# Queueing the third branch's weight sums early, and another split of the last output tile

## The chip, the cores and the metric

The kernel runs on one core of a Trainium2 chip. The metric is the device time of one execution in microseconds. The core has TensorE (PE in the profile) for matmuls, VectorE (DVE), ScalarE (ACT), GpSimd (POOL) and SyncE (SP); sixteen DMA engines move data between HBM and the on-chip memories. Here SP's queue loads weights and inputs, and POOL's queue carries transfers from HBM to HBM, some of which add to what stands at their destination.

## What is computed

One layer of an encoder on 512 tokens of width 1024, in float32. Three branches, each a half-width mixer of the same normalised input, are projected back to 1024 columns, weighted by sigmoid gates and summed; an output projection, a gated feed-forward part and a final norm follow.

```python
h = _rmsnorm(x, norm_mix[l])
p = h @ w_in[l]
u, v, bg, cg, xb, zc, gl = jnp.split(p, splits, axis=-1)
ya = _sgu(gelu(u), gelu(v), ...)
yb = bg * _causal_dwconv(cg * xb, conv_b_w[l])
yc = _pool_mixer(zc, pool_w[l], pool_scale[l])
g = jax.nn.sigmoid(gl).reshape(bn, s, N_BRANCH, D_MODEL)
merged = (g[:, :, 0] * (ya @ w_br_a[l])
          + g[:, :, 1] * (yb @ w_br_b[l])
          + g[:, :, 2] * (yc @ w_br_c[l]))
x = x + merged @ w_o[l]
h = _rmsnorm(x, norm_ffn[l])
a = _causal_dwconv(h @ w_up[l], ffn_conv_w[l])
ag, av = jnp.split(a, 2, axis=-1)
x = x + (silu(ag) * av) @ w_down[l]
return _rmsnorm(x, norm_f)
```

## The kernel before, in words

Every matmul is done in three passes: each operand is split into a rounded upper half and a remainder (`_hi`, `_lo`), and `mm3` (L81 to L83) multiplies upper by upper, upper by lower, lower by upper, 128 by 128 weights against 512 columns a time. Weights come from HBM in pieces of 512 KB, through SP's queue (L106), into a pool of raw buffers (at most four in use for the weights). ACT rounds a piece into `ring_hi` (L59, or L63 where the piece is negated), DVE takes the remainder into `ring_lo` (L67 or L64), and PE uses the pair. The ring has four slots, so the split of a piece waits for its load and for the product four pieces earlier to be through.

The order of the program is: the value input (`pv`), the columns of the input projection (`pu`, `pz`, `pcg`, `pxb`, `pbg`), then branch 0, gate 0, branch 1, gate 1, branch 2, gate 2 (`bx`, `bd`, `ba` for a branch; `gx`, `ga`, `gd` for a gate), the output projection (`po`), the feed-forward part (`pug`, `puv`) and the down projection (`dx` to `df`), whose tail scales the rows and stores them.

Branches, gates and the down projection are multiplied by Strassen's scheme: seven products of quarters in place of eight, of which four need sums of quarters of the weight. For the three gates, the third branch and the down projection these sums are made by DMA, without an engine: `WeightSums` (L135) keeps four tensors t1 to t4 in HBM, `copy` (L146) copies a quarter into each, and `add` (L151) adds another quarter, or an earlier sum, to it by an accumulating transfer. t2 gets t1 added to it, t4 gets t2. The first two branches make their sums on DVE from loaded quarters (`more`, L178).

POOL issues the sums' transfers in the order written (`in_order`). The sums of gates 0 and 1 are queued one after another at L635, once the value input is through. Those of the third branch (512 KB a transfer) and of gate 2 (1 MB a transfer) stand in a list, `behind` (L927 to L930), and `next_sum` takes one entry from it at certain products: ACT copies one column of the product's accumulator into a mark (L936), POOL copies that mark (L407, `passed`), and the transfers behind it start only then. `next_sum` is called after each of a gate's seven products, and, in branches 1 and 2, after the third product (L1039).

DVE and ACT work in the order written too. In a branch (L1028) the last product, `a22`, goes into the bank `x` that held `s3`, so it starts after DVE has taken `s3` out (L842). In the next branch's first steps, ACT copies `bx` (L951) into a scratch buffer that the gate before used for its last weighing on DVE (L842).

At the end, `finish` (L1216) scales a token tile of 1024 columns by its row factor `rstd`. Half of the columns is scaled by ACT and sent from ACT's queue (L1221, L1222); the other half by DVE and sent from SP's (L1225, L1228, L1229). In the last tile DVE does it in two pieces of 256 columns, of which one still needs the norm's gain.

Of the kernel before, what the change touches and what calls it, by code (L numbers as in the profile page):

```python
# [10 lines left out]
AF = mybir.ActivationFunctionType  # L11
ALU = mybir.AluOpType
# [7 lines left out]
NT = S // P  # L20
# [6 lines left out]
def trunk_kernel(  # L27
# [4 lines left out]
    nc = tc.nc  # L32
# [8 lines left out]
    def bank(name):  # L41
        return ps.tile([P, S], F32, tag="ps", name=name)

    def scratch(i, name, width=S):
        return scr.tile([P, 528], F32, tag=f"s{i}", name=name)[:, :width]
# [46 lines left out]
    class Raws:  # L92


        def __init__(self):
            self.todo, self.ready, self.live, self.cap = [], [], 0, 4
# [38 lines left out]
    class WeightSums:  # L135
        def __init__(self, name, b11, b12, b21, b22):
            t1, t2, t3, t4 = self.t = [
                dram.tile([P, b11.shape[1], 528], F32, name=f"{name}_t{i + 1}")[:, :, :512] for i in range(4)]
            self.base = [(t1, b11), (t3, b12), (t2, b22), (t4, b21)]
            self.added = [(t1, b12), (t3, b22), (t2, t1), (t4, t2)]  # L140

            self.products = {"m1": b11, "m2": b21, "m3": b22, "m4": t4, "m5": t1, "m6": t2, "m7": t3}

# [96 lines left out]
    def tiny(tag, name):  # L240
        return small.tile([P, 1], F32, tag=tag, name=name)
# [156 lines left out]
    def quarters(half, c0):  # L398
        return [half(k)[:, :, c0 + 512 * h:c0 + 512 * h + 512] for k in range(2) for h in range(2)]

    gate_sums = [WeightSums(f"g{i}", *quarters(lambda k: w_in_v[:, 4 * k:4 * k + 4], 3072 + 1024 * i))
                 for i in range(3)]
    last_branch_sums = WeightSums("br2", *quarters(lambda k: w_br_q[2][k], 0))

    def pool_waits_for(t, name):

        in_order(nc.gpsimd.tensor_copy(tiny(name, name), t[:, 0:1]))  # L407
# [25 lines left out]
    def load_gain(g, tags, name):  # L433

        halves = []
        for c in range(2):
            t = act.tile([P, S], F32, tag=tags[c], name=f"{name}{c}")
            nc.sync.dma_start(t, g[512 * c:512 * c + 512].partition_broadcast(P))
            halves.append(t)
        return halves  # L440
# [191 lines left out]
        v_gelu(t)  # L632
    v_center()
    pool_waits_for(pw_raw, "begun")
    for sums in gate_sums[:2]:  # L635
        sums.copy()
        sums.add()

# [25 lines left out]
    for b in range(2):  # L664
        w = blocks.take(f"u{b}")
        for j in range(2):
            o = bank(f"pu{b}{j}")
# [80 lines left out]
    for b in range(2):  # L748
        w = blocks.take(f"z{b}")
        for j in range(2):  # L750
            g = 2 * b + j
            o = bank(f"pz{g}")
# [7 lines left out]
    for b in range(2):  # L760
        w = blocks.take(f"cg{b}")
        cg = []
        for j in range(2):
            o = bank(f"pcg{b}{j}")
# [8 lines left out]
        for j in range(2):  # L773
            c = 2 * b + j
            o = bank(f"pxb{c}")
# [6 lines left out]
            a = scratch(1, f"cva{c}")  # L782
# [7 lines left out]
        for j in range(2):  # L790
            c = 2 * b + j
            o = bank(f"pbg{c}")
# [27 lines left out]
    def form(tags, name):  # L820

        return [[act.tile([P, 2, 256], F32R, tag=tags[2 * kp + i], name=f"{name}_{p}{kp}")
                 for i, p in enumerate(("hi", "lo"))] for kp in range(2)]
# [17 lines left out]
    def tt(o, a, b, op):  # L841
        nc.vector.tensor_tensor(o, a, b, op=op)  # L842
# [41 lines left out]
    sums = []  # L884
# [39 lines left out]
    nc.vector.tensor_scalar(nrstd1, rstd1, -1.0, None, op0=ALU.mult)  # L924


    behind = [lambda: last_branch_sums.copy()]  # L927
    behind += [lambda: last_branch_sums.add(1)] * 4
    behind += [lambda: gate_sums[2].copy(2)] * 2
    behind += [lambda: gate_sums[2].add(1)] * 4  # L930

    def next_sum(o):
        if behind:
            n = len(behind)
            mark = tiny(f"mark{n}", f"mark{n}")
            nc.scalar.copy(mark, o[:, 0:1])  # L936
            pool_waits_for(mark, f"passed{n}")
            behind.pop(0)()

    def product(o, st, n, first):  # L940
        for q in range(0, n, 2):
            [w] = pieces.take()
            for k in range(q, q + 2):
                mv = [p[:, 512 * (k - q):512 * (k - q) + 512] for p in w]
                for r in range(2):
                    mm3(o[r], st(k, r), mv, first and k == 0, k == n - 1, more=not first)

    def copies(tag, name, o):
        got = [scratch(tag, f"{name}{r}") for r in range(2)]
        for r in range(2):  # L950
            nc.scalar.copy(got[r], o[r])  # L951
        return got

    def banks(name):
        return [bank(f"{name}{r}") for r in range(2)]
# [72 lines left out]
    def branch(i, form):  # L1028
        c = [[act.tile([P, S], F32, tag=f"m{8 + 2 * t + h}" if i == 0 else f"x{t}{h}", name=f"c{i}{t}{h}")
              for h in range(2)] for t in range(NT)]  # L1030
        x = banks(f"bx{i}")
        product(x, form("a11"), 2, True)
        m1 = copies(0, f"bm1{i}", x)
        d = banks(f"bd{i}")
        product(d, form("s1"), 2, True)
        m5 = copies(1, f"bm5{i}", d)
        product(x, form("s2"), 2, False)
        if i > 0:
            next_sum(x[1])  # L1039
        m16 = copies(2, f"bm16{i}", x)  # L1040
        a = banks(f"ba{i}")
        product(a, form("a12"), 2, True)
        for r in range(2):
            tt(c[r][0], a[r], m1[r], ALU.subtract)
        product(x, form("s3"), 2, False)
        for r in range(2):
            tt(c[2 + r][1], x[r], m5[r], ALU.add)
        product(d, form("s4"), 2, False)
        for r in range(2):
            tt(c[r][1], d[r], m16[r], ALU.add)  # L1050
        product(x, form("a22"), 2, False)
        for r in range(2):
            nc.scalar.mul(c[2 + r][0], x[r], -1.0)
        return c

    for i in range(3):
        c = branch(i, forms[i])
        if i == 0:
            acc = c
        gate(i, c)  # L1060


    xr = [[act.tile([P, S], F32, tag=f"x{t}{c}", name=f"xr{t}{c}") for c in range(2)] for t in range(NT)]
# [11 lines left out]
    for h in range(2):  # L1075
        o = {}
# [88 lines left out]
    for b in range(NFF // 2):  # L1165
        w = blocks.take(f"ug{b}")
        ag = []
        o = [bank(f"pug{b}{j}") for j in range(2)]
# [13 lines left out]
        o = [bank(f"puv{b}{j}") for j in range(2)]  # L1182
# [6 lines left out]
    out_t = out[0].rearrange("(t p) d -> t p d", p=P)  # L1189

    def tail_rstd(ss, name):

        n = ss.shape[-1] - 1
        b = eps_t
        for i in range(n):
            b2 = tiny(f"b{i % 2}", f"{name}_b{i}")
            nc.vector.scalar_tensor_tensor(
                b2, ss[:, i:i + 1], 1.0 / D, b, op0=ALU.mult, op1=ALU.add)
            b = b2
        nb = tiny("nb", f"{name}_nb")  # L1200
        nc.vector.tensor_scalar(nb, b, -0.5, None, op0=ALU.mult)
        r = tiny("rr", f"{name}_r")
        nc.scalar.activation(r, ss[:, n:n + 1], AF.Sqrt, scale=1.0 / D, bias=b)
        h = tiny("rh", f"{name}_h")
        nc.vector.scalar_tensor_tensor(h, ss[:, n:n + 1], -0.5 / D, nb, op0=ALU.mult, op1=ALU.add)
        y = tiny("ry", f"{name}_y")
        nc.vector.reciprocal(y, r)
        t = tiny("rt", f"{name}_t")
        nc.vector.scalar_tensor_tensor(t, y, h, y, op0=ALU.mult, op1=ALU.mult)
        y2 = tiny("rz", f"{name}_z")  # L1210
        nc.vector.scalar_tensor_tensor(y2, t, 1.5, y, op0=ALU.add, op1=ALU.mult)
        return y2
# [3 lines left out]
    def finish(t):  # L1216

        h = int(t < 2)
        rstd = tail_rstd(ssf[t], f"hf{t}")
        xs = xr[t][1 - h]  # L1220
        nc.scalar.activation(xs, xs, AF.Copy, scale=rstd)  # L1221
        nc.scalar.dma_start(out_t[t][:, 512 * (1 - h):512 * (1 - h) + 512], xs)  # L1222
        a = 0 if t < NT - 1 else 256
        xs = xr[t][h][:, a:]
        nc.vector.scalar_tensor_tensor(xs, xs, rstd, gain3[h][:, a:], op0=ALU.mult, op1=ALU.mult)  # L1225
        if a:
            xs = xr[t][h][:, :a]
            nc.vector.tensor_scalar(xs, xs, rstd, None, op0=ALU.mult)  # L1228
        nc.sync.dma_start(out_t[t][:, 512 * h:512 * h + 512], xr[t][h])  # L1229

    def add_up(t, h, i, cut=slice(0, 512), gain=True):

# [49 lines left out]
    x = banks("dx")  # L1282
# [4 lines left out]
    gain3 = load_gain(norm_f, (g_tags[40], g_tags[41]), "gain_f")  # L1287
# [12 lines left out]
    a = banks("da")  # L1300
# [13 lines left out]
    for r in range(2):  # L1314
        tt(xr[r][1], d[r], m16[r], ALU.add)
        add_up(r, 1, 1, gain=False)
        finish(r)
# [5 lines left out]
    for qs in ([0], [2], [4, 6, 8, 10]):  # L1323
        ws = taken(qs)
        for r in range(2):
            t = 2 + r
            for i, (cut, o) in enumerate(zip(cuts[r], f[r])):
                o = o[:, :cut.stop - cut.start]
# [37 lines left out]
```

## Time and profile before

| | us |
|---|---|
| median of 3 runs (lowest, highest) | 739.06 (738.57, 740.81) |
| profiled execution: its own time | 736.67 |
| profiled execution: span from first to last instruction | 734.9 |
| PE busy in the span | 720.7 |
| DVE busy, ACT busy, POOL busy | 562.7, 370.6, 62.6 |

PE is the busiest engine. The page's busy time says nothing of stops by itself: the list of waits tells what PE waited for, the table by stretches tells where, and the chain of work and the timelines tell why. The profiled execution lies 2.4 us under the median of the runs, and 1.9 us under the lowest.

### The profile page before, as it was taken

How to read it: one execution, taken by the hardware profiler on the slowest of the kernel's cores; microseconds unless marked ns; L12 is line 12 of the kernel's file. 1: busy time of each engine (PE TensorE's matmuls, PEld its weight loads, DVE VectorE, ACT ScalarE, POOL GpSimd, SP SyncE). 2: the span in 40 equal slices, each digit the busy share in tenths (PEclk: the TensorE clock that was granted, in tenths of full speed). 3: DMA queues.
4: the chain of work that ended last, by engine and by line, in shares of the span. 5: the costliest groups of instructions: out<-in, count | busy, mean ns of one | idle time of the engine just before them, and what ended most of it. 6: DMA issues, size and time to landing. Idle time of an engine off the chain costs nothing.

```text
span 734.9 us, 8928 instructions
## 1 busy us (share of the span) xinstructions
PE 720.7 (98%) x3258; PEld 594.8 (81%) x3258; DVE 562.7 (77%) x836; ACT 370.6 (50%) x551; POOL 62.6 (9%) x93
## 2 busy tenths in 40 slices
PE   8999999999999998999999999999999999999996
PEld 5888888888877886888888888888888888888885
DVE  6889899889598687677556786766787776997674
ACT  4744144266675565664444443443444444965453
POOL 0041210001221100000012010100000000000110
PEclk9999999999999999999999999999999999999999
DMA  8649999737999996675228999999633232576652
GB/s 254 192 170 283 244 331 237 183 90 232 304 313 313 229 295 199 196 225 183 87 75 264 236 296 285 253 311 220 178 97 105 86 106 82 155 234 201 194 163 114
DMA packets 89211, 150.87 MB, mean 205 GB/s; under 512 B 4008, under 2 KB 39248, under 8 KB 89168
## 3 DMA queue, kind: packets, MB, share of 16 engines
q1 hardware_dynamic: 68607, 96.76, 41.7%
q0 software_dynamic: 19840, 52.43, 29.8%
q10 hardware_dynamic: 720, 1.11, 0.4%
q8 instruction: 25, 0.41, 0.2%
q14 instruction: 19, 0.15, 0.1%
HBM read 148.20 MB, written 54.53 MB: 276 GB/s over the span
## 4 chain that ended last, share of the span: by engine, by line
PE 93%; DVE 3%; DMA 2%; ACT 1%; issue 1%; SPq 0%; ACTq 0%
PE pug L83 5%; PE puv L83 5%; PE pug L81 5%; PE puv L81 5%; PE puv L82 5%; PE pug L82 5%; PE gx L82 3%; PE gx L81 3%; PE gx L83 3%; PE dx L83 2%; PE dx L82 2%; PE po L81 2%; PE dx L81 2%; PE po L83 2%; PE po L82 2%; PE gd L83 1%
## 5 line engine op out<-in xcount | busy, mean ns | idle before, releaser
L81 PE MATMUL pug<-h2T_hi,ring_hi 128*128 128x512 f32 x176 | 68.7, 390 | 0.0
L83 PE MATMUL pug<-h2T_hi,ring_lo 128*128 128x512 f32 x176 | 68.5, 389 | 0.0
L82 PE MATMUL puv<-h2T_lo,ring_hi 128*128 128x512 f32 x176 | 68.5, 389 | 0.0
L81 PE MATMUL puv<-h2T_hi,ring_hi 128*128 128x512 f32 x176 | 68.5, 389 | 0.0
L82 PE MATMUL pug<-h2T_lo,ring_hi 128*128 128x512 f32 x176 | 68.5, 389 | 0.0
L83 PE MATMUL puv<-h2T_hi,ring_lo 128*128 128x512 f32 x176 | 68.5, 389 | 0.0
L67 DVE TENSOR_TENSOR ring_lo<-raw_g_m,ring_hi 128x1024 fp32r<-128x1024 f32 x30 | 36.6, 1224 | 29.2 <-ACT ring_hi L59 29.1
L59 ACT CAST ring_hi<-raw_ug 128x1024 fp32r<-128x1024 f32 x22 | 23.3, 1057 | 47.4 <-PE pug L82 42.2
L67 DVE TENSOR_TENSOR ring_lo<-raw_uv,ring_hi 128x1024 fp32r<-128x1024 f32 x22 | 26.9, 1222 | 25.1 <-ACT ring_hi L59 25.1
L59 ACT CAST ring_hi<-raw_g_m 128x1024 fp32r<-128x1024 f32 x30 | 31.5, 1055 | 26.2 <-DMA raw_g_m<-in_w_in_dram 9.6
L67 DVE TENSOR_TENSOR ring_lo<-raw_d_m,ring_hi 128x1024 fp32r<-128x1024 f32 (+1 forms) x30 | 35.8, 1204 | 9.0 <-ACT ring_hi L59 8.9
L59 ACT CAST ring_hi<-raw_d_m 128x1024 fp32r<-128x1024 f32 (+1 forms) x30 | 29.5, 982 | 18.6 <-PE da L83 8.2
L82 PEld LDWEIGHTS puv<-h2T_lo,ring_hi 128*128 128x128 f32 x176 | 33.0, 188 | 6.9
L82 PEld LDWEIGHTS pug<-h2T_lo,ring_hi 128*128 128x128 f32 x176 | 33.0, 188 | 6.9
L83 PEld LDWEIGHTS pug<-h2T_hi,ring_lo 128*128 128x128 f32 x176 | 33.0, 188 | 6.9
L83 PEld LDWEIGHTS puv<-h2T_hi,ring_lo 128*128 128x128 f32 x176 | 33.0, 188 | 6.9
L81 PEld LDWEIGHTS puv<-h2T_hi,ring_hi 128*128 128x128 f32 x176 | 33.0, 188 | 6.9
L81 PEld LDWEIGHTS pug<-h2T_hi,ring_hi 128*128 128x128 f32 x176 | 33.0, 188 | 6.8
L67 DVE TENSOR_TENSOR ring_lo<-raw_ug,ring_hi 128x1024 fp32r<-128x1024 f32 x22 | 26.9, 1222 | 8.8 <-ACT ring_hi L59 8.7
L59 ACT CAST ring_hi<-raw_uv 128x1024 fp32r<-128x1024 f32 x22 | 23.2, 1056 | 19.1 <-PE puv L82 18.8
L1136 ACT ACTIVATE av<-av_y,colv 128x512 f32<-128x512 f32 x22 | 16.0, 727 | 27.9 <-DVE av_y L1134 26.9
L1136 ACT ACTIVATE ag<-ag_y,colv 128x512 f32<-128x512 f32 x22 | 15.8, 720 | 21.5 <-DVE ag_y L1134 21.5
(432 smaller groups left out, 2028.9 us busy)
## 6 DMA issues: line engine op xcount, KB each, us to landing
g_t<-in_w_in_dram POOLq DMA_DIRECT2D x18, 1024.0 KB, 13.2
d_t<-in_w_down_dram POOLq DMA_DIRECT2D x6, 2816.0 KB, 27.2
raw_g_m<-g_t SPq DMA_DIRECT2D x24, 512.0 KB, 4.2
raw_ug<-in_w_up_dram SPq DMA_DIRECT2D x22, 512.0 KB, 6.2
raw_uv<-in_w_up_dram SPq DMA_DIRECT2D x22, 512.0 KB, 5.1
raw_d_m<-d_t SPq DMA_DIRECT2D x20, 512.0 KB, 3.9
raw_g_m<-in_w_in_dram SPq DMA_DIRECT2D x18, 512.0 KB, 10.0
raw_d_m<-in_w_down_dram SPq DMA_DIRECT2D x15, 512.0 KB, 3.3
```

The costliest lines, as they stand in the source:

```text
L59: return keep(nc.scalar.copy(hi, src))
L67: return keep(nc.vector.tensor_tensor(lo, src, hi.bitcast(F32), op=ALU.subtract))
L81: keep(nc.tensor.matmul(o, st[0], mv[0], start=first, stop=False, **skip))
L82: keep(nc.tensor.matmul(o, st[0], mv[1], start=False, stop=False, **skip))
L83: keep(nc.tensor.matmul(o, st[1], mv[0], start=False, stop=last, **skip))
L1136: nc.scalar.activation(a, y, AF.Copy, scale=ffn_w(2, c))
```

## The change

- `WeightSums` now lists the transfers as t1, t2, t3, t4, for copies and for adds. Before, t3 stood ahead of t2 in both. This holds for the gates, the third branch and the down projection.
- The third branch's sums leave the list of marks. Their four copies and four adds are queued right behind those of gate 1.
- The list `behind` holds gate 2's sums alone: one copy at each of four marks, then one add at each of four. The mark in the branches (L1039) is dropped. There are 8 marks in place of 11.
- In the last token tile, the half that ACT scaled (512 columns, row factor alone) goes to DVE, ahead of DVE's other work, and is sent from SP's queue. ACT scales 256 columns of the other half, DVE 256 with the gain, and ACT's queue sends that half once both are done. The other three tiles keep their shares.

```diff
-            self.base = [(t1, b11), (t3, b12), (t2, b22), (t4, b21)]
-            self.added = [(t1, b12), (t3, b22), (t2, t1), (t4, t2)]
+            self.base = [(t1, b11), (t2, b22), (t3, b12), (t4, b21)]
+            self.added = [(t1, b12), (t2, t1), (t3, b22), (t4, t2)]
...
-    for sums in gate_sums[:2]:
+    for sums in gate_sums[:2] + [last_branch_sums]:
         sums.copy()
         sums.add()
...
-    behind = [lambda: last_branch_sums.copy()]
-    behind += [lambda: last_branch_sums.add(1)] * 4
-    behind += [lambda: gate_sums[2].copy(2)] * 2
+    behind = [lambda: gate_sums[2].copy(1)] * 4
     behind += [lambda: gate_sums[2].add(1)] * 4
...
         product(x, form("s2"), 2, False)
-        if i > 0:
-            next_sum(x[1])
...
         xs = xr[t][1 - h]
+        nc.vector.tensor_scalar(xs, xs, rstd, None, op0=ALU.mult)
+        nc.sync.dma_start(o[1 - h], xs)
+        xs = xr[t][h][:, :256]
         nc.scalar.activation(xs, xs, AF.Copy, scale=rstd)
...
+        xs = xr[t][h][:, 256:]
+        nc.vector.scalar_tensor_tensor(xs, xs, rstd, gain3[h][:, 256:], op0=ALU.mult, op1=ALU.mult)
+        nc.scalar.dma_start(o[h], xr[t][h])
```

How the change moves POOL's instructions is seen at two places. The first is behind the last add of gate 1's sums (`g1_t4`); `br2` is the third branch, L146 a copy, L151 an add. Before:

```order
L151 DMA g1_t4_120<-g1_t2_118 512x512
L407 COPY passed11_1643<-mark11_1641 128x1
L146 DMA br2_t1_125<-in_w_br_c_dram 256x1x512
L146 DMA br2_t3_127<-in_w_br_c_dram 256x1x512
L146 DMA br2_t2_126<-in_w_br_c_dram 256x1x512
L146 DMA br2_t4_128<-in_w_br_c_dram 256x1x512
L407 COPY passed10_1689<-mark10_1687 128x1
L151 DMA br2_t1_125<-in_w_br_c_dram 256x1x512
L407 COPY passed9_1732<-mark9_1730 128x1
L151 DMA br2_t3_127<-in_w_br_c_dram 256x1x512
```

With the change:

```order
L151 DMA g1_t4_120<-g1_t2_118 512x512
L146 DMA br2_t1_125<-in_w_br_c_dram 256x1x512
L146 DMA br2_t2_126<-in_w_br_c_dram 256x1x512
L146 DMA br2_t3_127<-in_w_br_c_dram 256x1x512
L146 DMA br2_t4_128<-in_w_br_c_dram 256x1x512
L151 DMA br2_t1_125<-in_w_br_c_dram 256x1x512
L151 DMA br2_t2_126<-br2_t1_125 256x512
L151 DMA br2_t3_127<-in_w_br_c_dram 256x1x512
L151 DMA br2_t4_128<-br2_t2_126 256x512
L407 COPY passed8_1651<-mark8_1649 128x1
L146 DMA g2_t1_121<-in_w_in_dram 512x1x512
```

No mark stands any more between gate 1's last add and the third branch's last add; the first mark of gate 0 now releases gate 2's first copy.

The second place is gate 2's sums (`g2`), on POOL again. Before, from the last mark but one of gate 0 on (marks 6 and 5 stand in gate 0, mark 4 in branch 1, marks 3 to 1 in gate 1):

```order
L407 COPY passed6_1899<-mark6_1897 128x1
L146 DMA g2_t1_121<-in_w_in_dram 512x1x512
L146 DMA g2_t3_123<-in_w_in_dram 512x1x512
L407 COPY passed5_1941<-mark5_1939 128x1
L146 DMA g2_t2_122<-in_w_in_dram 512x1x512
L146 DMA g2_t4_124<-in_w_in_dram 512x1x512
L407 COPY passed4_2023<-mark4_2021 128x1
L151 DMA g2_t1_121<-in_w_in_dram 512x1x512
L407 COPY passed3_2140<-mark3_2138 128x1
L151 DMA g2_t3_123<-in_w_in_dram 512x1x512
L407 COPY passed2_2183<-mark2_2181 128x1
L151 DMA g2_t2_122<-g2_t1_121 512x512
```

With the change, from the fourth mark of gate 0 on (marks 5 to 2 stand in gate 0, mark 1 in gate 1):

```order
L407 COPY passed5_1822<-mark5_1820 128x1
L146 DMA g2_t4_124<-in_w_in_dram 512x1x512
L407 COPY passed4_1863<-mark4_1861 128x1
L151 DMA g2_t1_121<-in_w_in_dram 512x1x512
L407 COPY passed3_1904<-mark3_1902 128x1
L151 DMA g2_t2_122<-g2_t1_121 512x512
L407 COPY passed2_1945<-mark2_1943 128x1
L151 DMA g2_t3_123<-in_w_in_dram 512x1x512
L407 COPY passed1_2138<-mark1_2136 128x1
L151 DMA g2_t4_124<-g2_t2_122 512x512
```

Gate 2's first three adds stand in gate 0 now, at the products where the third branch's last add and gate 2's copies stood; its last add stands at gate 1's first product in place of its third.

## Rows read from the trace of the kernel before

**Rows 1.** Head of the page: the span, and busy time of each engine.

```profile
span 734.9 us, 8928 instructions
...
PE 720.7 (98%) x3258; PEld 594.8 (81%) x3258; DVE 562.7 (77%) x836; ACT 370.6 (50%) x551; POOL 62.6 (9%) x93
```

**Rows 2.** What PE waited for: us in total, times, the longest.

```profile
PE bx L81 <- ACT bm L951: 3.3, 2, 2.7
PE bx L81 <- DVE c L842: 1.7, 1, 1.7
```

**Rows 3.** Stretches at the second stop: length, busy by engine, clock, DMA share, GB/s.

```profile
275.50:278.40 2.90, 0.19 (x2) 0.03 (x1) 2.90 (x6) 1.47 (x3) 0.00 (x0) 1.00 0.35 74
278.40:282.10 3.70, 3.70 (x9) 2.91 (x10) 3.40 (x3) 2.44 (x4) 0.00 (x0) 0.54 0.63 186
```

**Rows 4.** The same table by stage, in the stretch of the sums.

```profile
144.00:155.00 11.00, 11.00 (x50) 9.09 (x50) 10.15 (x14) 3.77 (x6) 0.00 (x0) 1.00 0.00 0
...
226.00:241.00 15.00, 13.28 (x59) 10.70 (x58) 12.58 (x18) 10.79 (x16) 1.38 (x2) 1.00 0.99 281
241.00:260.00 19.00, 19.00 (x85) 15.73 (x85) 10.46 (x12) 9.30 (x14) 2.25 (x5) 1.00 1.07 261
```

**Rows 5.** Chain of work through branch 1: start, us, what.

```profile
217.25 1.23 DVE raw_br_b L178
...
218.53 7.46 DMA raw_g_m<-in_w_in_dram
...
228.31 0.70 DVE c L842
```

**Rows 6.** Timelines of DVE, ACT and SP ahead of branch 2 (idle time and its releaser behind).

```profile
260.21 1.23 DVE L67 TENSOR_TENSOR ring_lo<-raw_g_m,ring_hi 128x1024 fp32r<-128x1024 f32 x1 [2.27 <-ACT ring_hi L59]
...
271.13 1.23 DVE L67 TENSOR_TENSOR ring_lo<-raw_br_m,ring_hi 128x1024 fp32r<-128x1024 f32 x1 [1.31 <-ACT ring_hi L59]
...
270.04 1.05 ACT L59 CAST ring_hi<-raw_br_m 128x1024 fp32r<-128x1024 f32 x1 [4.37 <-PE gx L82]
...
261.47 1.84 SPq L106 DMA_DIRECT2D raw_br_m<-br_t  x2
```

**Rows 7.** DMA issues and packets in short stretches (from 166, 243, 259, 228 us).

```profile
raw_g_m<-g_t SPq DMA_DIRECT2D x2, 512.0 KB, 3.5
...
raw_g_m<-in_w_in_dram SPq DMA_DIRECT2D x2, 512.0 KB, 13.0
g_t<-g_t POOLq DMA_DIRECT2D x1, 1024.0 KB, 15.1
...
g_t<-g_t POOLq DMA_DIRECT2D x1, 1024.0 KB, 10.3
...
q0 software_dynamic: 194, 0.40, 71.1%
q1 hardware_dynamic: 191, 0.39, 38.7%
```

**Rows 8.** Timeline of POOL: gate 1's last add, and three marks passed.

```profile
132.77 1.02 POOL L151 DMA_DIRECT2D g_t<-g_t  x1 [12.56 <-issue]
177.56 0.39 POOL L407 COPY passed<-mark 128x1 f32<-128x1 f32 x1 [43.77 <-ACT mark L936]
...
200.35 1.20 POOL L407 COPY passed<-mark 128x1 f32<-128x1 f32 x1 [3.64 <-ACT mark L936]
...
239.37 0.26 POOL L407 COPY passed<-mark 128x1 f32<-128x1 f32 x1 [15.85 <-ACT mark L936]
```

**Rows 9.** DMA issues of the page: the third branch's copies and first two adds together.

```profile
br_t<-in_w_br_c_dram POOLq DMA_DIRECT2D x6, 512.0 KB, 8.3
```

**Rows 10.** Last tile on DVE and ACT's queue, and a 512-column TENSOR_SCALAR.

```profile
730.77 0.35 DVE L1228 TENSOR_SCALAR xr<-xr,hf_z 128x256 f32<-128x256 f32 x1
...
731.18 0.34 ACTq L1222 DMA_DIRECT2D out_dram<-xr  x1
...
L783 DVE TENSOR_SCALAR cva<-cg,colv 128x512 f32<-128x512 f32 x4 | 1.9, 483 | 0.0
```

More of the change, by code (lines that the diff above doesn't have):

```diff
@@ L1219, in finish @@
         rstd = tail_rstd(ssf[t], f"hf{t}")
+        o = [out_t[t][:, 512 * i:512 * i + 512] for i in range(2)]
+        if t < NT - 1:
+            xs = xr[t][1 - h]
+            nc.scalar.activation(xs, xs, AF.Copy, scale=rstd)
+            nc.scalar.dma_start(o[1 - h], xs)
+            xs = xr[t][h]
+            nc.vector.scalar_tensor_tensor(xs, xs, rstd, gain3[h], op0=ALU.mult, op1=ALU.mult)
+            nc.sync.dma_start(o[h], xs)
+            return
         xs = xr[t][1 - h]
+        nc.vector.tensor_scalar(xs, xs, rstd, None, op0=ALU.mult)
+        nc.sync.dma_start(o[1 - h], xs)
+        xs = xr[t][h][:, :256]
         nc.scalar.activation(xs, xs, AF.Copy, scale=rstd)
[L1222 to L1229, printed above, removed]
+        xs = xr[t][h][:, 256:]
+        nc.vector.scalar_tensor_tensor(xs, xs, rstd, gain3[h][:, 256:], op0=ALU.mult, op1=ALU.mult)
+        nc.scalar.dma_start(o[h], xr[t][h])
     def add_up(t, h, i, cut=slice(0, 512), gain=True):
```

## The prediction

> **What bounds the kernel now.** I read the page's head first. PE is busy for 720.7 of 734.9 us [rows 1], so the time is PE's work and what stops it. No PE instruction but the order of its neighbours is touched by the change; it can gain only where PE stands still, or runs slowly. The list of what PE waited for has two entries in the stretch of the sums: ACT's copies of `bx` (two stops, 3.3 us, the longer 2.7) and DVE's `c` (one stop, 1.7 us) [rows 2]. The table by stretches puts the 2.7 us at 275.5 to 278.4 us, the third product of branch 2, and shows something more: in the 3.7 us behind it the granted clock is 0.54, a mean that lies close to the lower of TensorE's levels, 1.2 of 2.4 GHz [rows 3]. At 0.54 of full speed, 3.7 us lose 0.46 x 3.7 = 1.7 us. The 1.7 us stop lies in branch 1, and in the stretch from 226 us around it the clock stays at 1.00 [rows 4]. The other ACT stop, 3.3 - 2.7 = 0.6 us, is at the third product of branch 1. Together: 0.6 + 1.7 + 2.7 + 1.7 = **6.7 us that the stretch can give back at most**.
>
> What makes these stops? In branch 1 the chain of work is plain: DVE adds the last quarter (L178), which frees raw buffers; SP then loads the first piece of gate 1; that load takes 7.46 us; its split on DVE stands ahead of the `c` that PE's last product waits for [rows 5]. A load of the same size with the DMA engines to itself takes 3.5 us [rows 7]. In branch 2 the chain ends in ACT's copies, which wait for DVE, and DVE is late because ACT's rounding of the second `br_m` piece starts at 270.04 after 4.37 us idle [rows 6]. The row names PE's `gx` as releaser. I don't believe it: the slot was last read by gate 1's sixth product, which by the count of products ended some 5 us earlier (50 matmuls took 11 us [rows 4], so a product of 24 takes 5.3, and the seventh ends here). The other thing that this rounding waits for is its load, issued at 261.47 [rows 6]. It ran beside gate 2's last add, which was issued at 259.36 and took 10.3 us, so until 269.7 [rows 7]. That fits 270.04. I take both stops, then, as **late loads behind the sums' transfers**. The DMA share is 0.99 and 1.07 from 226 to 260 us, and 0.00 from 144 to 155 us [rows 4].
>
> **The change part by part.**
>
> *Third branch's sums, moved.* Eight transfers of 512 KB leave the marks of gate 0 and go behind gate 1's last add, issued at 132.77 [rows 8]. With that add landing some 12 us later (10.3 to 15.1, [rows 7]), at about 145, and four adds that follow each other, at 8.3 us each [rows 9], they end at about 145 + 4 x 8.3 = 178 at most; some overlap, so 170 is likelier. That is where the engines moved nothing for 11 us. The first mark of gate 0 is passed at 177.56 [rows 8], so POOL is hardly late for it. Loads issued from 155 us on get company that they had not. I cost this at nothing: they feed a ring that is ahead there (PE has no wait in that stretch, [rows 2]), and a load of 3.5 us that becomes 6 to 8 us still comes before its slot is free. If that cover is gone, a piece 2 us late stops PE for 2 us.
>
> *Gate 2's sums, moved forward.* Its copies now come one at a mark in gate 0; the first add goes out at the mark passed at 200.35, the second has to wait for the first (10.3 us, [rows 7]), so about 212, the third follows at once, and the fourth goes out at the mark passed at 239.37 [rows 8]. Two adds together take 15.1 us [rows 7]: second and third are in flight from 212 to about 228. The fourth, at 10.3, ends at 250. Before, the last add ended at 269.7. Loads for the end of gate 1 and for branch 2 (243 to 276 us) so lose their company: 13.0 us becomes nearer 3.5 [rows 7].
>
> What this is worth at the second stop: the load issued at 261.47 lands near 265, 5 us before 270. DVE then saves its 1.31 us idle at 271.13, and the 2.27 us at 260.21, where ACT's rounding had waited for a load too [rows 6]. Sum 3.6 us, against a stop of 2.7. DVE still has its own work, so I leave 0.4 us of stop: gain 2.3, bounds 1.3 (only the last idle time) and 2.7. A stop of 1.7 us was followed by full clock [rows 4], so with a short stop the 1.7 us of slow clock are gained too; bounds 0 and 1.7.
>
> At the first stop the company changes from copies to the second and third add. The price of a load behind two adds is unknown here. Bounds: 13.0 us, as the loads of 243 us had it, so 5.5 us later; or 3.5 us, as if alone, 4.0 earlier. Between: from 228 us on, with one add running, SP's queue (q1) moved 191 packets in 3 us and POOL's (q0) 194 [rows 7]. A 512 KB load is 256 packets of 2 KB, 4.0 us at that pace; q1's share of the engines was 38.7%, so with all of them it needs 0.387 x 4.0 = 1.6 us; 3.5 + 4.0 - 1.6 = 5.9 us. I take 5.9, since this load is the first in SP's queue, while those of 13.0 us had others ahead of them. That is 1.6 us earlier than 7.46, nearly the whole stop; I leave a rest and count a gain of 1.3 of the 1.7 us. The Trainium skill, page "DMA: Bandwidth & Descriptors", section "Queues, rings and completion order", says that each DMA engine takes turns between the queue rows that have work, a packet each; the two counts agree. The same section says that the completion mark of a transfer lands only after all earlier writes of that engine, across its queues, which speaks for the 13.0; the sum would be 5.5 us worse by it.
>
> Branch 1's short stop of 0.6 us: its own loads (195 to 208 us) have one copy and one add beside them in place of two adds; I take half, 0.3, bounds 0 and 0.6.
>
> *Marks.* Three one-column copies fewer on ACT and POOL, in their idle time: 0. *Order t1, t2, t3, t4* for the earlier gates and the down projection: one overlap of adds moves from (t1, t3) to (t3, t2); same bytes, and the sums are over long before they are used: 0.
>
> *Last tile.* DVE's 512-column scaling takes 0.48 [rows 10], by the four rows of the same form, where the 256-column one had 0.35, so the 256 columns behind it end some 0.1 us later, and ACT's queue sends at about 731.25 in place of 731.18 [rows 10]. The other half goes out 0.25 us earlier. Cost 0.1, bounds -0.3 and +0.3.
>
> **Sum.** 0.3 + 1.3 + 2.3 + 1.7 - 0.1 = 5.5 us. The profiled execution, 736.67, would be 731.2. The median of the runs is 2.4 us above the profiled time; I put the forecast against the median: 739.06 - 5.5 = **733.6 us**.
>
> **The rivals.** A measurement of this kernel can tell about 0.3%, 2.2 us, from no change.
>
> *A, the forecast:* both stops mostly gone, no slow clock, 4.5 to 6.7 us, 732.4 to 734.6. Chance 0.53.
>
> *B, half of it:* the second stop shrinks to a length that leaves the clock alone, the first stays as it is: 1.3 + 1.7 to 2.7 + 1.7, so 3.0 to 4.4 us, 734.7 to 736.1. For it: DVE is busy for 10.5 of 19 us before, but nearly all of the time right at the stop [rows 3, 4]. Chance 0.22.
>
> *C, no change:* the second stop is DVE's and ACT's own order, and the row that names PE is right. Then loads help only the first stop: 1.3 + 0.3 = 1.6 us, 737.5. Against it stands the count of products. Chance 0.14.
>
> *D, slower:* the two adds sit on gate 1's first loads. If the load issued at 218.53 lands at 231.5 (13.0 us) the stop of 1.7 us becomes 7.2, long enough for the clock to fall as after the 2.7 us stop: +5.5 + 1.7, less the 4.0 that the second stop and its clock give back, so +3.2 us, 742.3. It decides from the point where that load lands some 3 us later than the 226 of before. For it: the 13.0 row and the rule on completion marks; against it: the packet counts. Chance 0.08. The completion rule is borne out by no row here.
>
> *E, slower:* the moved sums delay branch 0's and gate 0's loads (155 to 178 us) beyond the ring's lead; three pieces 2 us late, 6 us lost against 5.5 gained, about 739.6, or 745 if the gain fails too. PE had no wait there at all. Chance 0.03.
>
> **How the numbers follow.** Faster by over 0.3% holds A and B, 0.75; within 0.3% is C and part of E, 0.16; slower D and the rest of E, 0.09. The range that holds 8 in 10 runs from A's best, 739.06 - 6.7 - 0.3 (tail) - 0.5 (lowest run under the median) = 731.6, up past B into C: 737.8.
>
> **What would show it.** POOL's copies of `br_t` at 134 to 138 us and its last add before 178; the DMA share of 144 to 155 us no longer 0.00; the last add of gate 2 issued near 240 in place of 259. Loads of branch 2 at 3.5 us. PE's list of waits without the 2.7 us, and no clock below 1.00 at 270 to 285 us. It is wrong if the wait for ACT's `bm` at branch 2 stays with loads on time (C), if gate 1's first load takes over 10 us and PE stops there for longer than before (D), or if PE waits for `ring_lo` between 150 and 180 us (E).

## The result, and the profile after

The change takes **730.53 us** (median of 4 runs, 730.25 to 731.02), the kernel before 738.82 (4 runs, 737.35 to 740.81): a ratio of 0.9887, 95% interval 0.9863 to 0.9911. It is faster, as forecast, by some 8 us where 5.5 were forecast, and the time lies 1.1 us below the range's low end (731.6).

The profiled execution took 731.02 us against 736.67. Between the two traces the gain is thus 5.65 us, and 731.2 was what the sum gave for that execution. Against the trace, then, the sum came out; what failed is the step from the trace to the median. Inside the sum single terms are off too, in opposite directions, as the rows show.

Head of the page of the change, to be read against [rows 1]:

```profile
span 729.2 us, 8924 instructions
...
PE 718.9 (99%) x3258; PEld 595.0 (82%) x3258; DVE 563.0 (77%) x836; ACT 370.4 (51%) x548; POOL 59.9 (8%) x90
```

PE's busy time falls by 1.8 us, about what the slow clock cost; the rest of the 5.7 us of span is mostly stops.

What PE waited for with the change (us in total, times, longest):

```profile
PE warm_ps L422 <- DVE warm L413: 1.6, 1, 1.6
PE bx L81 <- DVE c L842: 1.5, 1, 1.5
PE tp L454 <- DMA x<-in_x_dram: 0.9, 1, 0.9
```

Against [rows 2]: the two stops behind ACT's `bm`, 3.3 us, are gone. The stop behind DVE's `c` has hardly moved, 1.7 to 1.5. The other two rows are the program's start.

The table by stretches (columns as in [rows 3]: length, busy by engine, clock, DMA share, GB/s):

```profile
144.00:155.00 11.00, 11.00 (x50) 9.13 (x49) 10.15 (x13) 3.86 (x6) 2.91 (x3) 1.00 0.74 143
...
226.00:241.00 15.00, 13.47 (x60) 10.84 (x59) 12.87 (x18) 10.04 (x16) 1.49 (x2) 1.00 0.84 257
...
270.00:285.00 15.00, 15.00 (x68) 12.43 (x67) 11.82 (x15) 9.50 (x13) 0.00 (x0) 1.00 0.63 190
```

The third branch's sums fill the stretch that was idle (DMA share 0.00 to 0.74). In branch 2, 270 to 285 us, PE is busy all the time at a clock of 1.00, where [rows 3] had 2.7 us of stop and 3.7 us at 0.54.

POOL's timeline with the change (start, us, instruction, idle time before it and its releaser):

```profile
125.95 1.02 POOL L151 DMA_DIRECT2D g_t<-g_t  x1 [6.75 <-issue]
126.58 3.22 POOL L146 DMA_DIRECT2D br_t<-in_w_br_c_dram  x4
143.86 1.06 POOL L151 DMA_DIRECT2D br_t<-in_w_br_c_dram  x1 [14.07 <-DMA br_t<-in_w_br_c_dram]
...
157.21 0.89 POOL L151 DMA_DIRECT2D br_t<-br_t  x1 [4.40 <-issue]
178.15 0.39 POOL L407 COPY passed<-mark 128x1 f32<-128x1 f32 x1 [20.05 <-ACT mark L934]
...
200.15 1.19 POOL L151 DMA_DIRECT2D g_t<-in_w_in_dram  x1
205.35 1.20 POOL L407 COPY passed<-mark 128x1 f32<-128x1 f32 x1 [4.01 <-ACT mark L934]
211.93 1.06 POOL L151 DMA_DIRECT2D g_t<-g_t  x1 [5.37 <-DMA g_t<-in_w_in_dram]
...
213.51 1.15 POOL L151 DMA_DIRECT2D g_t<-in_w_in_dram  x1
...
239.58 1.02 POOL L151 DMA_DIRECT2D g_t<-g_t  x1
```

Nearly everything stands where it was forecast: last add of the third branch at 157, long before the first mark at 178; gate 2's second add (`g_t<-g_t`) held back 5.37 us by the first; its last add at 240 in place of 259. The third branch's copies went out at 127 and not at 134, since gate 1's last add was issued at 125.95 here and at 132.77 before [rows 8]. But see what follows from the 5.37 us: the second and third add go out 1.6 us apart, and 3 us later come gate 1's first loads.

DMA issues of two stretches of the change (KB, us from issue to landing), from 260.5 us and from 217 us:

```profile
raw_br_m<-in_w_br_c_dram SPq DMA_DIRECT2D x2, 512.0 KB, 3.8
...
raw_g_m<-in_w_in_dram SPq DMA_DIRECT2D x1, 512.0 KB, 11.4
```

These loads of branch 2 are nearly as quick as loads alone, 3.5 in [rows 7]. Gate 1's second load takes 11.4 us, near the 13.0 of [rows 7]. Branch 1 ahead of its stop (a row of ACT's timeline, then the chain of work: start, us, what):

```profile
225.31 1.06 ACT L63 ACTIVATE ring_hi<-raw_g_m 128x1024 fp32r<-128x1024 f32 x1 [4.68 <-PE bd L82]
...
226.40 1.23 DVE ring_lo L64
227.63 0.61 DVE c L842
228.38 0.47 PE bx L81
```

From the rounding on this is the chain of [rows 5]. The rounding's row names PE's `bd` as releaser, but it was the load: by its completion marks in the trace, gate 1's first piece, issued at 216.46, had landed whole at 225.23, 0.08 us ahead of the rounding, and the distance is 0.08 us in the kernel before too (225.99 and 226.07). The load took 8.77 us, 1.3 us more than the 7.46 of [rows 5]. It was issued 2.1 us earlier than there (218.53), as DVE's adding of the last quarter (L178) began at 215.18 here and at 217.25 in [rows 5]; so the stop stayed nearly as it was.

The last tile (timeline of DVE and of ACT's queue):

```profile
725.07 0.49 DVE L1227 TENSOR_SCALAR xr<-xr,hf_z 128x512 f32<-128x512 f32 x1
725.48 0.48 DVE L1232 SCALAR_TENSOR_TENSOR xr<-xr,hf_z,gain_f 128x256 f32<-128x256 f32 x1
...
726.04 0.34 ACTq L1233 DMA_DIRECT2D out_dram<-xr  x1
```

### The profile page after: what moved, and what is told of

It reads as the page before. It is cut to its first block, busy times and chain, and to the rows that moved or that the text cites. A ratio compares the mean times of both kernels' runs of the same rounds, so it can differ in the third digit from the quotient of the medians.

```text
span 729.2 us, 8924 instructions
## 1 busy us (share of the span) xinstructions
PE 718.9 (99%) x3258; PEld 595.0 (82%) x3258; DVE 563.0 (77%) x836; ACT 370.4 (51%) x548; POOL 59.9 (8%) x90
## 4 chain that ended last, share of the span: by engine, by line
PE 98%; DMA 1%; DVE 0%; ACT 0%; SPq 0%; issue 0%; DVEq 0%
PE puv L82 5%; PE pug L82 5%; PE pug L83 5%; PE pug L81 5%; PE puv L83 5%; PE puv L81 5%; PE gx L82 3%; PE gx L81 3%; PE gx L83 3%; PE dx L82 2%; PE dx L81 2%; PE po L81 2%; PE dx L83 2%; PE po L82 2%; PE po L83 2%; PE bx L81 2%
## 5 line engine op out<-in xcount | busy, mean ns | idle before, releaser
L1132 ACT ACTIVATE ag<-ag_y,colv 128x512 f32<-128x512 f32 x22 | 15.7, 717 | 21.5 <-DVE ag_y L1130 21.5
```

What stands on the lines that cost most here:

```text
L1132: nc.scalar.activation(a, y, AF.Copy, scale=ffn_w(2, c))
```

## The experiments

Three theories stood after the result. **L**: what PE waits for in branches 1 and 2 is late loads behind the sums' transfers. **V**: the stops of the kernel before vary from execution to execution, so that the profiled one, 2.4 us under the median, had less of them than most. **S**: the new order of gate 2's adds keeps the stop in branch 1. The rival of L is the prediction's C. Runs were made in jobs, each a batch on one chip with the kernel before among its runs; a ratio is to the kernel before of the same job.

**The kernel before, again, and a third trace of it.** No edit.

> The kernel before, unchanged, so that several of its executions are seen with their span and clock. Theory V (varying stops): the 2.4 us between its profiled execution (736.67) and its median (739.06) are no fixed offset but stops in branches 1 and 2 and the slow clock behind them, longer in some executions than in others; then its runs spread over 3 us or more, and the slower ones show a lower mean clock (0.990 to 0.995 in place of 0.996), while the changed kernel's four runs spread over 0.8 us at 0.998 to 0.999. Rival O (offset): runs differ by a start-up or end time alone; clock the same in all, within 0.001.

> The kernel before, unchanged, one more profiled execution, for the spread of its time (735.0 to 740.9 in 23 runs). Theory V (varying stops): time minus PE's stops in branches 1 and 2 and the slow clock is the same within 0.5 us as in the two executions at hand (736.67 with 0.7 + 1.9 + 2.9 us of stops; 737.63 with 0.6 + 2.2 + 3.1). Rival O (start and end vary): the stops are the same within 0.3 us and the rest differs.

The 12 runs of the first spread from 734.95 to 739.37 us, median 737.48; the other runs of the kernel before, beside the experiments, from 734.28 to 743.89. Sums alone, the change, and the two kernels with another order below stay within 2.8 us each. The third trace caught a long execution, 742.30 us. PE's waits in it, and its table by stretches behind two stops:

```profile
PE bx L81 <- ACT bm L951: 3.7, 2, 3.2
PE bx L81 <- DVE c L842: 3.3, 1, 3.3
```

```profile
232.00:236.00 4.00, 4.00 (x13) 3.08 (x12) 2.54 (x4) 1.39 (x3) 0.00 (x0) 0.60 1.10 266
...
284.00:288.00 4.00, 3.88 (x10) 3.11 (x11) 3.54 (x4) 2.56 (x5) 0.00 (x0) 0.58 0.62 194
```

The stop in branch 1 was 3.3 us here, against 1.7, and the clock fell behind it too. Cut at the first matmul of branch 0 and at the first of the output projection, the traces say where the variation lies (us):

| kernel | start to `bx` | `bx` to `po` | `po` to end |
|---|---|---|---|
| before, profiled at 736.67 | 152.66 | 180.91 | 401.29 |
| before, profiled at 737.63 | 153.46 | 181.12 | 401.23 |
| before, profiled at 742.30 | 153.63 | 185.60 | 401.29 |
| change, profiled at 731.02 | 153.25 | 174.95 | 401.03 |
| change, profiled at 730.81 | 152.48 | 175.47 | 401.06 |

The first part moves by about 1 us, the last by less than 0.1 within a kernel; the middle, branches and gates, moves by 4.7 us in the kernel before and by 0.5 in the change. Of the 5.6 us between the shortest and the longest of the three traces, 4.7 lie in the middle. So V holds for the long execution, and for the spread: the start and the end are much the same in all kernels here, yet the two kernels below whose traces have no stop in the middle stay within 1.6 us, in 4 and 8 runs, where the 74 runs of the kernel before spread over 9.6 us and the middle half of them over 2.7. For the distance from the first trace to the median it is argued, not shown: the trace at 737.63, close to its job's median, is 0.96 us longer than the first, and 0.80 of that is start and 0.21 middle. Nor does the slow clock tell the runs apart: the seven with a mean clock of 0.990 or 0.992 lie between 737.73 and 743.89 us, but those at 0.996 range from 734.95 to 739.63.

**The sums alone.** The change with the last tile of before put back.

```diff
-        nc.vector.tensor_scalar(xs, xs, rstd, None, op0=ALU.mult)
-        nc.sync.dma_start(o[1 - h], xs)
...
-        nc.scalar.dma_start(o[h], xr[t][h])
```

> The change without its last part: the last tile is scaled and sent as before. Theory L (late loads): nearly the whole gain is the sums' doing; the changed kernel's tail from DVE's last subtraction to the end is 6.2 us where before had 6.5, so 730.9 (0.3 above the changed kernel's 730.5). Rival T (the tail carries a part of the gain that the profiled execution hides): 732 or more.

731.31 us (6 runs), ratio 0.9925 (0.9906 to 0.9944) to the kernel before of its job, 737.77. Nearly the whole gain is the sums'.

**The last tile alone,** in the kernel before.

```diff
+        nc.vector.tensor_scalar(xs, xs, rstd, None, op0=ALU.mult)
+        nc.sync.dma_start(o[1 - h], xs)
...
+        nc.scalar.dma_start(o[h], xr[t][h])
```

> The kernel before with the change's last tile alone. Theory L: the stretch from the output projection to the end is 0.2 to 0.3 us shorter (401.0 for 401.3), the time is within noise of the kernel before, 735 to 740. Rival T: 2 us or more faster.

738.63 us, ratio 1.0009 (0.9990 to 1.0029): nothing that runs can tell. The traces can: from `po` to the end, this kernel took 401.07 us, and the six others with this tile 401.02 to 401.06, against 401.23 to 401.29 in the six without it. It gains 0.2 us.

**The third branch's sums moved, all else as before.** Old order, gate 2's sums at their old marks.

```diff
-    for sums in gate_sums[:2]:
+    for sums in gate_sums[:2] + [last_branch_sums]:
...
-    behind = [lambda: last_branch_sums.copy()]
-    behind += [lambda: last_branch_sums.add(1)] * 4
+    behind = [lambda: None] * 5
```

> The kernel before with the third branch's sums queued behind gate 1's, order t1 t3 t2 t4 and all marks and gate 2's sums as they were (five marks release nothing). Theory L: gate 2's last adds still run until about 270 us beside the loads of gate 1's end and of branch 2, so the stop at branch 2's third product and the slow clock behind it stay: 736 to 739. Rival M (moving the third branch's sums is what counts, since it takes 17 us of transfers out of gate 0): 731 to 732, no slow clock.

734.77 us (12 runs), ratio 0.9969 (0.9955 to 0.9983), 3.0 us less than the kernel before of its job, between what the two theories had. PE's waits and its table by stretches, in branch 2:

```profile
PE bx L81 <- ACT bm L950: 2.2, 1, 2.2
...
PE bx L81 <- DVE c L842: 0.4, 1, 0.4
```

```profile
273.00:276.00 3.00, 0.77 (x3) 0.32 (x3) 3.00 (x6) 1.57 (x3) 0.00 (x0) 1.00 0.45 104
276.00:279.00 3.00, 3.00 (x8) 2.34 (x7) 2.70 (x3) 2.15 (x4) 0.00 (x0) 0.50 0.53 156
```

The third branch's transfers were what stopped branch 1: both of its stops nearly go (0.4 us, where the traces of the kernel before have 1.7 to 3.3; none, where they have 0.4 to 0.6). Branch 2's stop stays, and the slow clock behind it. That one is gate 2's, as the next kernel shows.

**Gate 2's last two adds left out,** in the kernel before. Gate 2's sums t2 and t4 are then incomplete; the loads that use them read as much as before.

```diff
-    behind += [lambda: gate_sums[2].add(1)] * 4
+    behind += [lambda: gate_sums[2].add(1)] * 2
```

> The kernel before, with the last two adds of gate 2's sums (t2 and t4) left out, so gate 2's weight sums are incomplete; nothing else moves. Theory L (late loads): without these adds the loads of 243 to 276 us come in 3.5 to 5 us, the stop of 2.7 us at branch 2's third product goes or falls under 1 us, the clock stays 1.00 behind it, the stop of branch 1 stays: 733 to 734.5. Rival C (DVE's and ACT's own order makes the stop): the 2.7 us and the slow clock stay, 737 to 738.

734.05 us (7 runs), ratio 0.9950 (0.9921 to 0.9979). PE's waits, and the stretches of branch 1's stop and of branch 2:

```profile
PE bx L81 <- DVE c L842: 2.5, 1, 2.5
...
PE bx L81 <- ACT bm L951: 0.2, 1, 0.2
```

```profile
226.00:241.00 15.00, 12.50 (x55) 10.06 (x54) 11.10 (x16) 8.79 (x12) 0.00 (x0) 1.00 0.97 270
...
270.00:285.00 15.00, 15.00 (x68) 12.40 (x67) 12.02 (x15) 9.66 (x14) 0.00 (x0) 1.00 0.65 199
```

With engines, order and marks unchanged, and only two transfers gone, branch 2's stop and its slow clock are gone; branch 1's, ahead of them, stays. L holds and C falls: the row that named PE's `gx` as releaser [rows 6] was wrong. The completion marks in the two traces say the same: the load issued at 261.47 in the kernel before landed whole at 269.94, 0.10 us ahead of the rounding at 270.04, after 8.5 us; here the same load took 5.1.

**The old order.** The change with t3 ahead of t2 again, in all sums; and then in gate 2's alone. The change itself and the first of the two were run once more, in one job.

```diff
-            self.base = [(t1, b11), (t2, b22), (t3, b12), (t4, b21)]
-            self.added = [(t1, b12), (t2, t1), (t3, b22), (t4, t2)]
+            self.base = [(t1, b11), (t3, b12), (t2, b22), (t4, b21)]
+            self.added = [(t1, b12), (t3, b22), (t2, t1), (t4, t2)]
```

> The change with the transfers in the old order t1, t3, t2, t4. Theory L: bytes and places are the same but for one overlap of adds; t3 goes beside t1's end or at once, t2 waits for t1 as before: 730 to 731.5. Rival Q (the order is what counts, as it decides what is in flight at gate 1's first loads): 733 or more, with a stop of over 3 us in branch 1.

> The change, with gate 2's sums alone in the old order t1, t3, t2, t4; all others in the new. Theory S (second add waits): only gate 2's order counts, since its second add then starts at its mark near 206 us and not after the first add has landed near 212, so one add less is in flight at gate 1's first loads: 729.0 as with the old order everywhere, no stop of 1.5 us in branch 1. Rival E (the earlier gates' order counts, by what it leaves in flight at 100 to 150 us): 730.5, stop as in the change.

> The changed kernel, unchanged, on the same chip and beside the two that follow. Theory V: its stops in the middle are short (1.5 us), so its runs spread by 1 to 2 us and the median lies within 1 us of its profiled execution: 730 to 731.5, and 6.5 to 8 us under the kernel before (some 737.6 by 39 runs). Rival O: 2 us or more between its median and its profiled execution.

> The change with the old order t1, t3, t2, t4, again, now beside the change itself. Theory S (second add waits for the first): 1.2 to 2 us under the change, no stop in branch 1 or 2. Rival: the 1.5 us between the two earlier jobs was the chip's, the two agree within 0.5 us.

The old order took 729.02 us (4 runs), ratio 0.9893 (0.9869 to 0.9916), less than either theory had it. In one job, the change took 730.77 (729.90 to 732.18, 6 runs) and the old order 729.30 (728.82 to 729.87, 4 runs): 1.5 us, and the two sets of runs don't overlap. With gate 2's order alone turned back it is 729.30 too (729.09 to 730.70, ratio 0.9872, 0.9844 to 0.9901). So S holds, and the order of the other sums is worth nothing that runs can tell. The old order is also the best version of all: it beats the kernel before and the change.

PE's waits with the old order hold no row of a branch or a gate:

```profile
PE warm_ps L422 <- DVE warm L413: 1.6, 1, 1.6
PE tp L454 <- DMA x<-in_x_dram: 0.9, 1, 0.9
```

Why is in POOL's timeline of the old order:

```profile
199.95 1.19 POOL L151 DMA_DIRECT2D g_t<-in_w_in_dram  x1
205.15 1.21 POOL L407 COPY passed<-mark 128x1 f32<-128x1 f32 x1 [4.01 <-ACT mark L934]
206.30 1.17 POOL L151 DMA_DIRECT2D g_t<-in_w_in_dram  x1
...
211.81 1.04 POOL L151 DMA_DIRECT2D g_t<-g_t  x1 [0.18 <-issue]
```

The second add needs nothing of the first, so it starts at its mark, 206.30, while the first still runs. With the change it is t2, which waits for t1 until 211.93. The table by stretches, of the change and then of the old order, shows what the wait leaves idle:

```profile
207.00:216.00 9.00, 9.00 (x41) 7.48 (x40) 9.00 (x11) 7.49 (x13) 2.73 (x3) 1.00 0.62 111
```

```profile
207.00:216.00 9.00, 9.00 (x41) 7.48 (x40) 9.00 (x10) 7.50 (x14) 2.55 (x3) 1.00 1.12 222
```

111 GB/s against 222 in the 9 us ahead of gate 1's first loads: the bytes not moved there are moved beside the loads. Packets of POOL's queue (q0) and SP's (q1) from 221 to 223 us, again of the change and then of the old order:

```profile
q0 software_dynamic: 128, 0.26, 70.4%
q1 hardware_dynamic: 128, 0.26, 39.2%
```

```profile
q1 hardware_dynamic: 409, 0.78, 102.5%
q0 software_dynamic: 8, 0.01, 2.8%
```

In both kernels the first packet of gate 1's first piece moved 3.3 us after its issue, and only POOL's queue moved packets until then. Then, with the change, the queues share alike; with the old order the adds are all but over, and the loads have the engines to themselves. The rounding of gate 1's first piece (ACT's timeline) and the second load (DMA issues from 217 us), in the old order:

```profile
222.95 1.06 ACT L63 ACTIVATE ring_hi<-raw_g_m 128x1024 fp32r<-128x1024 f32 x1 [2.52 <-DMA raw_g_m<-in_w_in_dram]
```

```profile
raw_g_m<-in_w_in_dram SPq DMA_DIRECT2D x1, 512.0 KB, 6.8
```

The first piece was issued at 216.26 here and took 6.6 us, with the change 8.8; its rounding began 0.08 us behind it in both. The second took 6.8 in place of 11.4.

**No marks at all.** The old order, with gate 2's sums too queued behind the third branch's, `behind` empty.

```diff
-    for sums in gate_sums[:2] + [last_branch_sums]:
+    for sums in gate_sums[:2] + [last_branch_sums, gate_sums[2]]:
...
-    behind = [lambda: gate_sums[2].copy(1)] * 4
-    behind += [lambda: gate_sums[2].add(1)] * 4
+    behind = []
```

> Old order, and gate 2's sums without marks too: all four sets queued one behind the other, so gate 2's run from some 166 to 215 us, beside gate 0's loads. Theory L: gate 0's loads (half of them late already with adds beside them) come some 4 us later each; the ring leads by some 3 to 5 us there, so stops of 0 to 2 us in gate 0, none in branch 2: 729 to 731. Rival W (the marks hold nothing up that matters): 728.5 to 729, as the old order with marks.

741.35 us (10 runs), slower than the kernel before by a ratio of 1.0055 (1.0029 to 1.0080): both expectations were far off. The largest row of PE's waits in gate 0:

```profile
PE gd L82 <- DVE ring_lo L67: 2.5, 4, 0.8
```

The loads of gate 0 (DMA issues from 176 to 200 us), without marks and then in the old order with marks:

```profile
raw_g_m<-g_t SPq DMA_DIRECT2D x4, 512.0 KB, 13.2
```

```profile
raw_g_m<-g_t SPq DMA_DIRECT2D x4, 512.0 KB, 6.8
```

And the stretch of gate 0 and branch 1's beginning, in the same two kernels:

```profile
165.00:211.00 46.00, 41.18 (x170) 30.99 (x169) 25.18 (x33) 20.42 (x28) 3.44 (x4) 1.00 1.05 310
```

```profile
165.00:211.00 46.00, 46.00 (x204) 38.09 (x204) 37.75 (x48) 29.57 (x44) 7.96 (x13) 1.00 0.93 299
```

Loads take twice as long, and PE is busy for 41.18 of 46 us in place of all of it, with 170 matmuls in place of 204. From `bx` to `po` it needs 187.42 us against 173.15. This is the mechanism of the prediction's rival E, once 4 MB of copies and four adds of 1 MB are let loose on gate 0; the third branch's sums, half as large and earlier, do no such harm.

## Why the prediction was right and where it failed

- *What bounds the kernel.* Right: only PE's stops and the slow clock behind one of them moved. Against [rows 2, 3], the trace gave back 2.7 and 0.6 us of stops, 0.2 of the 1.7 us stop, and the clock's 1.7: 5.2 of the 6.7 us that were up. In the table above the middle part gives back 5.96 and the last 0.26, while the start is 0.59 longer: 5.6 in all. The middle gives back more than the rows because a stop costs some 0.3 us more than its row says: with the old order, which has no stop, the middle took 173.15 us in both traces; with the change, whose rows have one stop of 1.5 and of 2.1 us, 174.95 and 175.47. So "6.7 us that the stretch can give back at most" was too low even between traces: 180.91 - 173.15 = 7.8.
- *Third branch's sums: 0.* The cover was there (no wait between 150 and 180 us, the last add issued at 157.21). But they were not worth 0: moved by themselves they gained 3.0 us, as what they stopped before was branch 1. The prediction gave the third branch's adds a part in the short stop alone, 0.3, and expected the 1.3 in branch 1 from gate 2's copies giving way to its adds.
- *Second stop: 2.3, and its clock: 1.7.* Right in mechanism: the stop stays where gate 2's adds stay, and goes where the last two are left out. 2.7 and 1.7 measured.
- *Branch 1's short stop: 0.3.* Measured 0.6: no stop is left there.
- **"I take 5.9 ... count a gain of 1.3 of the 1.7 us."** Failed: the load took longer than before, 8.77 us, and the gain was 0.2. The pace was right: beside two adds, too, SP's queue moved 128 packets in 2 us, so 4.0 us for 256. What was too small is the rest, 3.5 - 1.6 = 1.9 us in the sum and 4.8 measured, of which 3.3 passed before the first packet moved. This is rival D's mechanism, in small: it stayed short of a longer stop because the load went out 2.1 us earlier.
- **The order of gate 2's adds** has no term in the sum. "Same bytes ... 0" is said of the earlier gates and the down projection; for these the runs can tell no difference, as turning back gate 2's order alone gives the same 729.30 as turning back all. For gate 2 the working had both facts (the second add waits until 212, two adds in flight until 228) and did not ask what the old order would do with the marks moved: the new one costs 1.5 us. What counts is not when the sums are used, but when they are in flight.
- *Last tile: −0.1.* Gained 0.2: DVE's last instruction and ACT's send are where they were put, but the last send, 0.22 us later after the last subtraction, landed 0.42 sooner (2.17 us against 2.59). Inside its bounds.
- **"The median of the runs is 2.4 us above the profiled time; I put the forecast against the median."** This is the step that failed, and it took the time out of the range. It carries the 2.4 us over whole, as a fixed distance, but the change's median lies 0.5 us below its own profiled execution: together 2.9 of the 3.1 us between 733.6 and 730.53. Part of the 2.4 was the luck of three runs, as later medians of the kernel before lie only 0.8 to 1.8 us above that trace. The rest goes, by the spreads above, mostly with the stops in the middle, which are longer in other executions (742.30: 3.3 and 3.2 us, slow clock twice) and which the change mostly takes away; how much of the median's own distance they are, no trace shows. The range reached down only 0.5 us for the spread of the runs.
- *The doubted releaser.* Disbelieving the row that named PE's `gx` was right; the count of products and the landing of an add beside it were better evidence, and the two adds left out settle it, with the load's own completion marks. The rule on completion marks ("DMA: Bandwidth & Descriptors", "Queues, rings and completion order", of the Trainium skill) stays undecided: no run separated it from plain sharing.

## What to carry to other kernels

Where a kernel's runs spread, look for stops that vary: the spread can be part of what a change that removes them gives back, so a forecast is better made against the time without the stops than by taking one trace's stops off the median. Of transfers that depend on each other, put an independent one second, so that the wait for the first does not push the others together and onto the loads that follow. And moving transfers into an idle stretch pays only as far as the stretch is idle: the same step with gate 2's sums, without marks, cost 12 us.

## What was not expected of the hardware

- In these traces the clock does not follow the length of a stop alone. It fell to 0.50, the lower of its two levels, for 3 us behind a stop of 2.2 us in branch 2 (third branch's sums moved), and to a mean of 0.60 for 4 us behind one of 3.3 us in branch 1 (third trace of the kernel before), but stayed at 1.00 to 241 us behind one of 2.5 us in branch 1 (two adds left out). What else decides was not tried.
- A load that SP issued while POOL's sums were in flight moved its first packet late: gate 1's first piece 3.1 to 3.5 us after its issue in six traces, beside two copies, two adds or one. With no other transfer running it was 1.0 to 1.3 us (four loads in the two shorter traces of the kernel before).
- A load of 512 KB took 3.8 us without sums beside it. With another load ahead of it in SP's queue it took 6.8 us beside one add for most of the time, and 11.4 beside two. The adds took 9.3 and 15.7 us for the pair with the change, the second beside the first and then beside the loads, and 10.1 and 10.3 with the old order.
